# A transformer layer on one core: output products in 256-column pieces, rank offsets moved to TensorE, static expert transfers reordered

## The chip, the core and the metric

One core of a Trainium2 chip runs the whole kernel. The metric is the device time of one execution in microseconds, the median of several runs; the profile is of one further execution. Engines are named as the profile does: PE (TensorE), DVE (VectorE), ACT (ScalarE), POOL (GpSimd), SP (SyncE, which issues nearly all transfers).

## The reference

One layer on 256 tokens of width 1024, all float32: an adaptive modulation by a condition vector `c`, a mixer of two halves (a gated linear recurrence and an attention of 8 heads), a deepnorm residual, and a mixture of 32 experts of which each token takes two.

```python
mod = (silu(c) @ w_ada + b_ada).reshape(6, 1024)        # sh1, sc1, g1, sh2, sc2, g2
u   = normalize(x) * (1 + sc1) + sh1
proj = u @ w_in                                         # x_lru, y_lru, q, k, v
mix = concat(rmsnorm(rg_lru(conv(x_lru)) * gelu(y_lru)),
             rmsnorm(attention(q, k, v))) @ w_out
x   = layernorm(ALPHA * x + g1 * mix)
u2  = normalize(x) * (1 + sc2) + sh2
# router: best of 4 groups, best 2 of its 8 experts, weights from both softmaxes
hdn = silu(u2 @ w1[e]) * (u2 @ w3[e])                   # e: 32 experts, 1024 -> 256
ffn = sum over a token's two experts of weight * (hdn @ w2[e])
out = layernorm(ALPHA * x + g2 * ffn)
```

## The kernel before

The kernel is written in the order in which each engine is to run its instructions; nothing reorders them. The 256 tokens are two halves of 128 (`i` = 0, 1), one token to a partition. Products are float32 on PE; one of 512 columns is two recorded matmuls.

**First part.** Modulation columns, the input projection, the recurrence and the attention. Weights come in transfers of 1 MB, issued by SP one after the other; each waits until the buffer it writes is free, and everything behind it on SP waits too. `mod2_out`/`mod2_in` send two modulation vectors to memory and back in another shape, both on SP: `mod2_in` waits until `mod2_out` has landed. `vec_mm(4, q, pa2)` and `vec_mm(5, q, pa2)` (line 597) form the modulation rows sc2 and g2 from a 2 MB weight each; all go to one PSUM bank, `pa2`, and `vec_rows` (L608) reads the first half of it on DVE.

**Middle part**, where the change is. For each half of the tokens, `base(i, h)` multiplies the recurrence's rows by the upper part of `w_out` (columns `h`*512 on), `wo_mm(i, h, 1)` (L815) the attention's rows by the lower part, and `z_half` (L906 to L908) adds the second into `xt` and takes statistics of the sum; `x2_of` then applies the first layernorm. `logits` and `top` find each token's two experts (`om`, one-hot rows, and `mb`, their sum in bfloat16). A token's rank within its expert is `mb` of the tokens before it, summed by a product with a triangular matrix (`trib`, L1084 for half 0, L1140 to L1142 for half 1). `early_slots(i, ranks)` adds each expert's offset `v512` to the ranks (L1073) and turns them into the one-hot matrix `ohs[:, i]` (L1074 to L1077), and `early_rows(i)` (L1081) gathers the tokens' rows with it by TensorE into the columns of the first expert product `products(ph0, first, xs0)` (L1223). Between them stand `acc_init(i, h)` (L1111), products that put ALPHA times the residual into the four accumulators in which the result is summed later.

**The experts.** Six experts are chosen before the router has run, by the router's bias (`early_experts`). They are called static, and `statics((e, part), ...)` issues their weights (part 0, 1, 2 is w1, w3, w2, 1 MB each) from L870 into buffers as they come free: experts 0 to 4, and w2 of all six, into buffers of earlier weights, w1 and w3 of expert 5 into `fifth`, which takes the place of `mT` and `lnb`. The order of these calls in the program is SP's order. When half 1's router is done, DVE finds which other experts have tokens (to `eof`, L1192), SP loads their numbers into registers, and `bring_all` (L1177, L1180) issues their weights one after the other into the buffers of experts that have been used. The first such transfer overwrites w1 of expert 0, so it waits until `products(ph0, ...)` has used it. `unit` then runs eight groups of experts; the last ends with the second layernorm and the stores.

Two rules of the framework matter below. A wait is for a count of instructions that another engine has finished. A bank of PSUM is one tile for this purpose: who reads any part of it waits until the last write that stands ahead of the read in the program.

## Time and profile before

| | |
|---|---|
| median of 3 runs | 305.39 us (305.02 to 308.27) |
| profiled execution, its own time | 306.72 us |
| its span in the trace | 304.9 us |
| busy share of PE / DVE / ACT | 92% / 60% / 36% |
| transfers | 112.24 MB, mean 368 GB/s |
| granted TensorE clock, mean | 0.981 of full |

The profiled execution took 1.3 us more than the median of the timed runs, and 1.82 us of its time lie outside the span. All positions below are microseconds from the start of the span.

### The profile page before, as it was taken

How to read it: one execution, taken by the hardware profiler on the slowest of the kernel's cores; microseconds unless marked ns; L12 is line 12 of the kernel's file. 1: busy time of each engine (PE TensorE's matmuls, PEld its weight loads, DVE VectorE, ACT ScalarE, POOL GpSimd, SP SyncE). 2: the span in 40 equal slices, each digit the busy share in tenths (PEclk: the TensorE clock that was granted, in tenths of full speed). 3: DMA queues.
4: the chain of work that ended last, by engine and by line, in shares of the span. 5: the costliest groups of instructions: out<-in, count | busy, mean ns of one | idle time of the engine just before them, and what ended most of it. 6: DMA issues, size and time to landing. Idle time of an engine off the chain costs nothing.

```text
span 304.9 us, 6238 instructions
## 1 busy us (share of the span) xinstructions
PE 279.5 (92%) x2408; PEld 187.1 (61%) x2408; DVE 184.0 (60%) x450; ACT 109.2 (36%) x230; POOL 29.0 (9%) x60
## 2 busy tenths in 40 slices
PE   0699999999999999999979999999999999978980
PEld 0578887998867644565556568575647464824430
DVE  2684597728775866897797791545263616250392
ACT  1233569497556352150455331214112311220111
POOL 0100037700010000001020200000000000400000
PEclk9999999999999999999997999999999999997996
DMA  7999999999997999699889699999999999999304
GB/s 284 427 420 421 419 416 416 396 419 421 419 420 291 383 397 416 213 392 347 318 293 412 255 411 422 422 421 418 422 418 420 422 419 420 419 417 400 122 3 148
DMA packets 18740, 112.24 MB, mean 368 GB/s; under 512 B 2253, under 2 KB 3586, under 8 KB 6156
## 3 DMA queue, kind: packets, MB, share of 16 engines
q1 hardware_dynamic: 18000, 110.74, 89.8%
q10 hardware_dynamic: 636, 0.99, 0.9%
q8 instruction: 21, 0.34, 0.4%
q14 instruction: 19, 0.16, 0.2%
q0 software_dynamic: 64, 0.01, 0.0%
HBM read 110.51 MB, written 1.22 MB: 366 GB/s over the span
## 4 chain that ended last, share of the span: by engine, by line
PE 63%; DMA 20%; DVE 11%; ACT 2%; issue 1%; POOL 0%; SPq 0%; ACTq 0%; DVEq 0%
PE b L425 15%; DMA arena<-in_w 12%; PE m L1223 10%; PE b L815 7%; DMA misc<-in_w 7%; PE m L1366 5%; PE b L790 4%; PE m L1297 3%; PE a L589 2%; PE a L1223 2%; PE acc L1320 2%; PE a L372 2%; PE a L601 2%; DMA pka<-in_pack_a 2%; PE acc L1111 1%
## 5 line engine op out<-in xcount | busy, mean ns | idle before, releaser
L425 PE MATMUL b<-ul,w 128*128 128x256 f32 x384 | 49.4, 287 | 0.6 <-ACT w L405 0.5
L425 PEld LDWEIGHTS b<-ul,w 128*128 128x128 f32 x384 | 46.9, 192 | 4.7 <-ACT w L405 1.4
L1223 PE MATMUL m<-arena,xg 128*64 128x256 f32 (+1 forms) x288 | 38.4, 401 | 3.3 <-DMA arena<-in_w 3.3
L403 DVE TENSOR_TENSOR w<-arena,w 128x512 fp32r<-128x512 f32 x32 | 21.9, 701 | 14.9 <-ACT w L402 14.7
L1223 PEld LDWEIGHTS m<-arena,xg 128*64 128x64 f32 (+1 forms) x288 | 21.9, 130 | 13.6 <-DMA arena<-in_w 4.2
L1366 PE MATMUL m<-arena,hT 128*32 128x512 f32 (+2 forms) x184 | 29.1, 596 | 0.5 <-ACT hT L1344 0.5
L815 PE MATMUL b<-arena,mT 128*128 128x512 f32 x64 | 29.0, 601 | 0.1
L1338 DVE TENSOR_TENSOR hh<-hh,m 128x256 f32<-128x256 f32 x7 | 3.0, 421 | 34.2 <-ACT hh L1337 34.2
L1223 PE MATMUL m<-fifth,xg 128*32 128x256 f32 (+1 forms) x96 | 23.2, 401 | 0.0
L402 ACT ACTIVATE w<-arena 128x512 fp32r<-128x512 f32 x32 | 19.4, 626 | 6.4 <-PE b L425 5.3
L1223 PE MATMUL m<-misc,xg 128*32 128x256 f32 (+1 forms) x160 | 21.3, 380 | 0.0
L1379 ACT ACTIVATE yh<-ys 128x256 fp32r<-128x256 f32 (+1 forms) x22 | 10.5, 493 | 29.8 <-DVE ys L1378 25.9
L815 PEld LDWEIGHTS b<-arena,mT 128*128 128x128 f32 x64 | 11.6, 190 | 13.1 <-issue 12.6
L1378 DVE SCALAR_TENSOR_TENSOR ys<-m,ws,g2b 128x256 f32<-128x256 f32 (+1 forms) x22 | 12.0, 578 | 12.1 <-PE m L1366 11.9
L1337 ACT ACTIVATE hh<-m 128x256 f32<-128x256 f32 x7 | 2.7, 384 | 45.8 <-PE m L1223 45.8
L1366 PEld LDWEIGHTS m<-arena,hT 128*32 128x32 f32 (+2 forms) x184 | 8.5, 120 | 16.7 <-issue 13.5
L1297 PE MATMUL m<-oh,xa 128*128 128x256 f32 (+1 forms) x64 | 15.6, 284 | 0.0
L1297 PE MATMUL m<-oh,xb 128*128 128x256 f32 (+1 forms) x64 | 15.4, 281 | 0.0
L1223 PE MATMUL m<-last,xg 128*32 128x256 f32 x64 | 14.2, 380 | 0.0
L1223 PEld LDWEIGHTS m<-fifth,xg 128*32 128x32 f32 (+1 forms) x96 | 11.7, 124 | 3.5 <-issue 1.4
L1223 PEld LDWEIGHTS m<-misc,xg 128*32 128x32 f32 (+1 forms) x160 | 13.3, 126 | 0.8
L739 ACT ACTIVATE s<-s,z 128x128 f32<-128x128 f32 (+1 forms) x16 | 7.1, 448 | 18.2 <-DVE z L737 18.2
(316 smaller groups left out, 501.7 us busy)
## 6 DMA issues: line engine op xcount, KB each, us to landing
arena<-in_w SPq DMA_DIRECT2D x41, 1024.0 KB, 13.8
arena<-in_w_ada SPq DMA_DIRECT2D x22, 1024.0 KB, 14.6
arena<-in_w_in SPq DMA_DIRECT2D x10, 1024.0 KB, 15.2
last<-in_w SPq DMA_DIRECT2D x6, 1024.0 KB, 14.2
misc<-in_w SPq DMA_DIRECT2D x6, 1024.0 KB, 13.8
fifth<-in_w SPq DMA_DIRECT2D x6, 1024.0 KB, 14.8
arena<-in_w_out SPq DMA_DIRECT2D x4, 1024.0 KB, 9.0
arena<-in_w SPq DMA_DIRECT2D x8, 512.0 KB, 12.7
```

Source lines behind the costliest of these rows:

```text
L372: te.matmul(pa[32 * j:32 * j + 32, 0:128], cd[:, k], V1[v, a][:, k, j * 128:(j + 1) * 128], start=(k == 0), stop=(k == KD - 1), skip_group ...
L402: se.activation(t[:, 0], w[:, k], AF.Copy)
L403: ve.tensor_sub(t[:, 1], w[:, k], t[:, 0])
L425: te.matmul(half(bs, m), t[:, a, m * 128:(m + 1) * 128], ul[:, b, k], start=(k + m % 2 + a + b == 0), stop=(k == KD - 1 and a == 1), skip_ ...
L739: se.activation(s3[:, c], s3[:, c], AF.Exp, bias=z[:, c:c + 1], accum_out=z[:, 4 + c:5 + c])
L790: te.matmul(pvv[i], ul[:, ua, k, i * 128:(i + 1) * 128], t[:, wa], start=(k + wa + ua == 0), stop=(k == KD - 1 and wa == 1))
L815: te.matmul(p, mT[:, k, i * 128:(i + 1) * 128], wo[k // 4][:, k % 4, h * 512:(h + 1) * 512], start=(m == 0), stop=(m == 3))
L1223: te.matmul(ph[o:o + w, a * 256:(a + 1) * 256], xs[:, k, o:o + w], place[q][0].rearrange("p (a k f) -> p a k f", a=2, k=KD)[:, a, k], star ...
L1297: te.matmul(q, nhl[i][:, a, k * 128:(k + 1) * 128], oh[:, i, :n], start=(a + i == 0), stop=(a + i == 2))
L1366: te.matmul(ps[h][o:o + w], hT[:, j, o:o + w], place[q][1][:, j * 1024 + h * 512:j * 1024 + (h + 1) * 512], start=(j == 0), stop=(j == 1), ...
L1378: ve.scalar_tensor_tensor(ys[:, o:o + q], p[:, o:o + q], ws, g2b[:, sl], op0=OP.mult, op1=OP.mult)
L1379: se.activation(yh[:, sl], ys[:, o:o + q], AF.Copy)
```

## The change

It does seven things.

- `w_out` is stored with its 512-column halves apart, so that the first MB of each part holds the columns of `h` = 0 for all rows and the second those of `h` = 1, where before each MB held all columns of half the rows. The static transfers that overwrite it can then be issued half by half.
- The output products of half 1, `wo_mm(1, h, 1)`, run as two pieces of 256 columns. Between the two pieces of `h` = 0 stands the triangular product for half 0's ranks (L1084 before).
- The offsets `v512` come into the ranks by a product of a row of ones with `v512` on PE, ahead of the triangular product in the same sum, in place of the addition on DVE (L1073). Half 1's ranks with offsets get columns of their own (96 to 128).
- `early_slots(0)` on DVE stands ahead of both `z_half(1, h)`. `z_half(1, 1)` works in two pieces of 256 columns, and the statistics of half 1 are taken over pieces of 256.
- `vec_mm(5, 0)` moves up, to behind `vec_mm(4, 1)`; `pv_mm(1, 0)` moves down behind `vec_mm(5, 1)`.
- `acc_init(1, 1)` moves from ahead of `early_rows(1)` to behind `products(ph0, ...)`.
- On SP, `mod2_in(rows0)` moves behind the loads of the two g2 weights and of the layernorm rows, and the static transfers come in another order.

```diff
-    r["w_out"] = np.stack([wo[:, 4 * j:4 * j + 4].reshape(128, 4096) for j in range(2)])
+    r["w_out"] = np.stack([wo[:, 4 * j:4 * j + 4].reshape(128, 4, 2, 512).transpose(0, 2, 1, 3).reshape(128, 4096) for j in range(2)])
...
-    mod2_in(mod2_out(rows1[64:128:32], 0), 0)
+    rows0 = mod2_out(rows1[64:128:32], 0)
...
-    def wo_mm(i, h, part, pool=None):
+    def wo_mm(i, h, part, pool=None, halves=(slice(0, 512),), mid=None):
         p = bank(pool)
-        for m in range(4):
-            k = 4 * part + m
-            te.matmul(p, mT[:, k, i * 128:(i + 1) * 128], wo[k // 4][:, k % 4, h * 512:(h + 1) * 512],
-                      start=(m == 0), stop=(m == 3))
+        for n, q in enumerate(halves):
+            if mid and n:
+                mid()
+            for m in range(4):
+                te.matmul(p[:, q], mT[:, 4 * part + m, i * 128:(i + 1) * 128], wo[part][:, h, m, q],
+                          start=(m == 0), stop=(m == 3), skip_group_check=len(halves) > 1)
         return p
...
     ve.memset(lg, NEG)
+    mod2_in(rows0, 0)
...
+    def z_half(i, h, b, st, mv, parts=None):
+        w = D // st.shape[1]
+        for q in parts or (slice(0, 512),):
+            o = slice(h * 512 + q.start, h * 512 + q.stop)
+            t = tmp.tile([128, 512], F32, name="s")[:, q]
+            ve.scalar_tensor_tensor(t, b[:, q], ra[:, i:i + 1], g1b[:, o], op0=OP.mult, op1=OP.mult)
+            ve.tensor_add(xt[:, i, o], xt[:, i, o], t)
+            for c in range(o.start, o.stop, w):
+                ve.bn_stats(st[:, c // w], xt[:, i, c:c + w])
...
     vec_mm(4, 1, pa2)
+    vec_mm(5, 0, pa2)
     rows2 = mod2_out(vec_rows(4, pa2)[0:128:32], 1)
     statics((1, 0), (1, 1))
     mod2_in(rows2, 1)
+    statics((2, 0), (2, 1))
...
-    vec_mm(5, 0, pa2)
-    statics((2, 0), (2, 1))
-    pv_mm(1, 0)
     vec_mm(5, 1, pa2)
...
     statics((3, 0), (3, 1))
+    pv_mm(1, 0)
     pt(1, 2)
     norm(1, 3)
     base(1, 0)
+    statics((0, 2))
...
     pl0 = raw_mm(0, zT0)
+    te.matmul(pl0[:, 64:96], onesf[0:1], v512[0:1], start=True, stop=False, skip_group_check=True)
     constants_mm()
...
-    statics((4, 0), (4, 1), (0, 2), (1, 2))
+    statics((4, 0), (4, 1), (1, 2))
     rms_cols(row, ra[:, 1:2], psp)
-    bs = [wo_mm(1, 0, 1, psx)]
+    bs = [wo_mm(1, 0, 1, psx, quarters, lambda: te.matmul(pl0[:, 64:96], trib, mb[:, 0], start=False, stop=True,
+                                                          skip_group_check=True))]
+    statics((2, 2))
...
-        ve.tensor_add(s2[:, i], ranks, v512)
-        ve.tensor_mul(omv[:, :, i], om[:, :, i], s2[:, i:i + 1].to_broadcast([128, 2, NE]))
+        ve.tensor_mul(omv[:, :, i], om[:, :, i], ranks[:, None, :].to_broadcast([128, 2, NE]))
...
-    te.matmul(pl0[:, 64:96], trib, mb[:, 0], start=True, stop=True)
-    bs.append(wo_mm(1, 1, 1, psx))
-    zs = z_start()
+    bs.append(wo_mm(1, 1, 1, psx, quarters))
+    early_slots(0, pl0[:, 64:96])
+    zs = z_start(4)
     z_half(1, 0, bs[0], *zs)
-    early_slots(0, pl0[:, 64:96])
     pgs = [bank(psp) for _ in range(2)]
     early_rows(0)
-    statics((2, 2), (3, 2))
-    z_half(1, 1, bs[1], *zs)
+    statics((3, 2))
+    z_half(1, 1, bs[1], *zs, quarters)
...
-    statics((4, 2), (5, 0), (5, 1), (5, 2))
+    statics((5, 0), (5, 1), (4, 2), (5, 2))
...
     p = bank(psp)
+    te.matmul(p[:, 96:128], onesf[0:1], v512[0:1], start=True, stop=False)
+    te.matmul(p[:, 96:128], oneb, mb[:, 0], start=False, stop=False)
+    te.matmul(p[:, 96:128], trib, mb[:, 1], start=False, stop=True)
...
-    for h in range(2):
-        acc_init(1, h)
+    acc_init(1, 0)
...
-    early_slots(1, rk[:, 1])
+    early_slots(1, p[:, 96:128])
...
     products(ph0, first, xs0)
+    acc_init(1, 1)
```

Where the instructions stand, at three places. First DVE at half 1's sum: `s<-b` is the output product times its scale, `xt<-xt,s` the addition, `bst` or `bsz` the statistics, `omv`, `sl` and `wsd` the slots of half 0. In brackets are the engines whose counts an instruction waits for. Before:

```order
L908 BN_STATS bst<-xt 128x6 [waits DVE_49]
L1073 TENSOR_TENSOR s_1643<-b,v_709 128x32 [waits PE_49]
L1074 TENSOR_TENSOR omv<-keepers,s_1643 128x2x32 [waits DVE_49]
L1075 TENSOR_REDUCE sl_1642<-omv 128x2 [waits DVE_49]
L1076 TENSOR_SCALAR wsd<-pkb,sl_1642 128x128 [waits DVE_49]
L1077 SCALAR_TENSOR_TENSOR wsd<-pkb,sl_1642,wsd 128x128 [waits DVE_49]
L906 SCALAR_TENSOR_TENSOR s<-b,ra,xb 128x512 [waits PE_49]
L907 TENSOR_TENSOR xt<-xt,s 128x512 [waits DVE_49]
L908 BN_STATS bst<-xt 128x6 [waits DVE_49]
```

The same place on DVE in the changed kernel:

```order
L1087 TENSOR_SCALAR wsd<-pkb,sl_1649 128x128 [waits DVE_49]
L1088 SCALAR_TENSOR_TENSOR wsd<-pkb,sl_1649,wsd 128x128 [waits DVE_49]
L913 SCALAR_TENSOR_TENSOR s<-b,ra,xb 128x512 [waits PE_49,Pool_49]
L914 TENSOR_TENSOR xt<-xt,s 128x512 [waits DVE_49]
L916 BN_STATS bsz<-xt 128x6 [waits DVE_49]
L916 BN_STATS bsz<-xt 128x6
L913 SCALAR_TENSOR_TENSOR s<-b,ra,xb 128x256 [waits PE_49]
L914 TENSOR_TENSOR xt<-xt,s 128x256 [waits DVE_49]
L916 BN_STATS bsz<-xt 128x6 [waits DVE_49]
L913 SCALAR_TENSOR_TENSOR s<-b,ra,xb 128x256
L914 TENSOR_TENSOR xt<-xt,s 128x256 [waits DVE_49]
L916 BN_STATS bsz<-xt 128x6 [waits DVE_49]
```

The slots stand ahead of the sum; the three operations on the second 512 columns have become six on 256. The first 256-column operation waits for PE and the second has no wait for PE of its own: both read one bank, and the one wait is for the last of the products written to it.

Second, PE around `vec_mm`: `a<-arena,cd` and `a<-last,cd` are the g2 products (16 matmuls to one `vec_mm`), `b<-arena,mT` the output products, `b<-pka,misc` transposes of the attention. Before:

```order
L601 MATMUL a<-arena,cd 32x256 x16
L760 MATMUL b<-pka,misc 128x128 x4
L808 MATMUL b<-avg,row 128x1
L815 MATMUL b<-arena,mT 128x512 x4
L760 MATMUL b<-pka,misc 128x128 x4
L725 MATMUL b<-nx 128x256 x4
L815 MATMUL b<-arena,mT 128x512 x8
L601 MATMUL a<-arena,cd 32x256 x16
L772 MATMUL b<-misc,xb 64x128 x8
L601 MATMUL a<-last,cd 32x256 x16
L1033 MATMUL a<-misc,pka 32x256 x4
L760 MATMUL b<-pka,misc 128x128 x4
```

The same place on PE in the changed kernel:

```order
L601 MATMUL a<-arena,cd 32x256 x32
L760 MATMUL b<-pka,misc 128x128 x4
L808 MATMUL b<-avg,row 128x1
L817 MATMUL b<-arena,mT 128x512 x4
L760 MATMUL b<-pka,misc 128x128 x4
L725 MATMUL b<-nx 128x256 x4
L817 MATMUL b<-arena,mT 128x512 x8
L601 MATMUL a<-last,cd 32x256 x16
L1040 MATMUL a<-misc,pka 32x256 x4
L772 MATMUL b<-misc,xb 64x128 x8
L760 MATMUL b<-pka,misc 128x128 x4
```

Sixteen g2 matmuls have moved ahead of three output products (12 of 512 columns); the work up to the last row is the same.

Third, PE from the ranks of half 1 to the gather `b<-wsd,nx`: `acc` is an `acc_init`. Before:

```order
L1141 LDWEIGHTS oneb
L1141 MATMUL b<-mb,oneb 128x32
L1142 LDWEIGHTS trib
L1142 MATMUL b<-mb,trib 128x32
L1111 MATMUL acc_1702<-xt,aid 128x512
L1111 MATMUL acc_1703<-xt,aid 128x512
```

The same place on PE in the changed kernel:

```order
L1154 LDWEIGHTS oneb
L1154 MATMUL b<-mb,oneb 128x32
L1155 LDWEIGHTS trib
L1155 MATMUL b<-mb,trib 128x32
L1121 MATMUL acc_1715<-xt,aid 128x512
L1092 MATMUL b<-wsd,nx 128x128 x8
```

One of the two `acc_init` is gone from ahead of the gather.

## Rows read from the trace of the kernel before

**Rows 1.** The page, part 2: memory traffic in 40 slices of 7.62 us.

```profile
GB/s 284 427 420 421 419 416 416 396 419 421 419 420 291 383 397 416 213 392 347 318 293 412 255 411 422 422 421 418 422 418 420 422 419 420 419 417 400 122 3 148
```

**Rows 2.** The chain that ended last: start, duration, what.

```profile
128.92 0.59 PE b L760 x4
...
142.80 3.54 PE b L815 x8
...
148.66 0.10 DVE s L1073
...
149.97 0.72 DVE s L906
...
152.17 0.22 DVE bmv L896
...
159.91 0.20 DVE mb L993
...
160.40 3.51 PE acc L1111 x4
163.91 1.78 PE b L1081 x16
165.69 7.17 PE a L1223 x128
...
182.47 6.92 PE m L1223 x32
...
219.50 15.74 DMA arena<-in_w
...
275.54 8.78 PE m L1223 x122
```

**Rows 3.** SP's timeline: transfers issued, start and duration.

```profile
97.89 0.86 SPq L233 DMA_DIRECT2D arena<-in_w_ada  x2
...
169.30 1.64 SPq L1177 DMA_DIRECT2D arena<-in_w  x3
```

**Rows 4.** SP's waits, 160 to 176 us: sum, times, longest.

```profile
SPq L1177 <- PE a L1223: 2.3, 2, 1.7
```

**Rows 5.** Windows of 4 us: busy by engine, PE clock, DMA share, GB/s.

```profile
168.00:172.00 4.00, 4.00 (x80) 2.44 (x76) 3.52 (x9) 0.19 (x1) 1.43 (x3) 1.00 0.43 124
...
276.00:280.00 4.00, 4.00 (x48) 2.08 (x44) 0.00 (x0) 0.00 (x0) 0.00 (x0) 0.57 1.03 401
```

**Rows 6.** DVE's groups by form: busy us, mean ns; idle before, releaser.

```profile
L1378 DVE SCALAR_TENSOR_TENSOR ys<-m,ws,g2b 128x256 f32<-128x256 f32 x14 | 6.1, 479 | 4.2 <-PE m L1366 4.1
...
L1385 DVE TENSOR_TENSOR yl<-ys,yh 128x256 fp32r<-128x256 f32 x14 | 5.3, 419 | 0.0
...
L906 DVE SCALAR_TENSOR_TENSOR s<-b,ra,xb 128x512 f32<-128x512 f32 x4 | 3.0, 751 | 4.6 <-PE b L815 2.4 <-PE b L1084 2.2
...
L907 DVE TENSOR_TENSOR xt<-xt,s 128x512 f32<-128x512 f32 x4 | 2.8, 692 | 0.1
```

**Rows 7.** DVE's timeline: start, duration.

```profile
126.52 0.70 DVE L750 TENSOR_TENSOR misc<-s,z 128x512 f32<-128x512 f32 x1
...
142.10 0.19 DVE L993 TENSOR_TENSOR mb<-keepers 128x32 bf16<-128x32 f32 x1
...
163.66 0.15 DVE L1192 TENSOR_SCALAR eof<-eid 128x1 int32<-128x1 f32 x1
164.91 1.37 DVE L1209 TENSOR_SCALAR xt<-b,mod2p 128x128 f32<-128x128 f32 x4 [1.10 <-PE b L1081]
```

**Rows 8.** PE's timeline: start, duration (recorded twice for each float32 matmul).

```profile
123.67 1.93 PE L601 MATMUL a<-arena,cd 128*32 128x256 f32 x32
...
134.11 0.38 PE L972 MATMUL b<-wsum,onesf 128*128 128x36 f32 x2
134.42 0.41 PE L973 MATMUL b<-pkb,onesf 1*128 1x36 f32 x2
```

**Rows 9.** PE in windows of 0.5 us: busy, granted clock, DMA share, GB/s.

```profile
163.00:163.50 0.50, 0.50 (x2) 0.50 1.08 459
```

More of the change, by code (lines that the diff above doesn't have):

```diff
@@ L248, in load_wo @@
     def load_wo(j, s):
-        return load(s, w_out[j], 4)
+        return load(s, w_out[j], 4).rearrange("p (h a) (b n) -> p h (a b) n", h=2, b=2)
     se.dma_start(pka, pack_a)
@@ L898, in bn_end, with z_start @@
         return mv, rs
-    def z_start():
-        return tmp.tile([128, 2, 6], F32, name="bst"), tmp.tile([128, 2], F32, name="bmv", bufs=4)
-    def z_half(i, h, b, st, mv):
-        sl = slice(h * 512, (h + 1) * 512)
-        t = tmp.tile([128, 512], F32, name="s")
-        ve.scalar_tensor_tensor(t, b, ra[:, i:i + 1], g1b[:, sl], op0=OP.mult, op1=OP.mult)
-        ve.tensor_add(xt[:, i, sl], xt[:, i, sl], t)
-        ve.bn_stats(st[:, h], xt[:, i, sl])
+    def z_start(n=2):
+        return tmp.tile([128, 4, 6], F32, name="bsz")[:, 0:n], tmp.tile([128, 2], F32, name="bmv", bufs=4)
+    quarters = (slice(0, 256), slice(256, 512))
+    def z_half(i, h, b, st, mv, parts=None):
[7 more added lines that the diff above has]
+                ve.bn_stats(st[:, c // w], xt[:, i, c:c + w])
     def x2_of(i, mv, rs):
```

## The prediction

> **What bounds the kernel now.** I read the memory traffic first [rows 1]: from slice 23, at 175 us, to slice 35 it stands at 409 to 422 GB/s without a gap. In the chain that ended last [rows 2] the pieces from 219.50 are transfers, and PE's last expert starts at 275.54, when its weights have landed. So the end comes a fixed time after the first transfer of a router-chosen expert. It is issued at 169.30 [rows 3]; SP stood ready and waited up to 1.7 us for PE [rows 4], for the first half of `products(ph0)`: that starts at 165.69 and takes 7.17 [rows 2], so its first half ends at 169.28. Between 168 and 172 memory moves only 124 GB/s [rows 5]: the static transfers are through, nothing else may start. Hence one number decides: how far **the start of `products(ph0)`** moves. Before it the chain [rows 2] is PE to the end of the output products (142.80, twice 3.54, the small triangular product between: 149.93), DVE from 149.97 to half 1's experts (159.91 + 0.20), then PE: two `acc_init` (3.51), the gather (1.78).
>
> **`vec_mm(5, 0)` earlier.** Its 16 matmuls, 1.86 us (32 of the recorded ones fill 123.67 to 125.60 [rows 8]), now stand ahead of three output products. PE's sum up to the transposes at 128.92 [rows 2] stays, but DVE gets its inputs 1.86 later. Those transposes need DVE's L750, done at 126.52 + 0.70 = 127.2 [rows 7]; now 129.1, so PE waits near 0.1. The same lateness follows through the next transposes and ACT's copies, which I put at another 0.1. Bounds: 0.1 and 0.5; I take **+0.2**. Its weight is asked for at 97.89 [rows 3]; 2 MB at 420 GB/s are 5 us, and the product now starts near 111, so it is there. DVE's lateness also reaches `mb` of half 0, ready at 142.29 [rows 7]; even with 1.86 on it that is 144.15, and PE reaches the triangular product, now in the middle of the first output product, at 142.80 + 1.77 = 144.57. Covered; what it costs without the cover is a rival below.
>
> **Offsets by PE, half 0.** A product of one row by 32 columns is added on PE's path. The nearest rows are two small ones whose starts are 0.31 apart [rows 8]: **+0.3**, bounds 0.1 and 0.4.
>
> **Output products in pieces.** Eight products of 512 columns, 0.885 each (3.54 for four), become 16 of 256. The trace has 16 full-array products of 256 columns in 6.92 [rows 2], 0.433 each, weight loads hidden. So 16 pieces cost 6.92 where the eight cost 7.08: **-0.1**, bounds -0.16 and +0.2. Together PE ends these products 0.4 later, near 150.3.
>
> **Slots of half 0 ahead of the sum.** On DVE they filled 148.66 to 149.97 [rows 2], and moving them looks like 1.3 us. But PE's last output product ends at 149.93 and DVE starts on it at 149.97: both came at the same time. The gain is **0.04**; DVE is only ready earlier and waits for PE.
>
> **The sum in pieces on DVE.** Could it start on the first 256 columns while PE makes the second? In the order of the changed kernel the first piece waits for PE and the second has no wait, so the one wait covers the bank's last product. DVE thus starts where it did, with six operations instead of three. The three took 152.17 - 149.97 = 2.20 [rows 2], 0.73 a step. An operation of 256 columns is shorter by 0.27 (0.751 against 0.479, 0.692 against 0.419 [rows 6]), so a step is 0.46 and six are 2.78: **+0.58**. For statistics of 256 columns no row exists; between half their 0.70 and all of it the bounds are +0.4 and +1.1, and I stay with the two forms that were measured. [...] The statistics of the first 512 columns are split too, but DVE has near 1 us to spare there.
>
> So DVE reaches half 1's statistics, and by unchanged steps its experts, 0.4 + 0.58 = **1.0 later**, at 161.1.
>
> **Offsets by PE, half 1.** The addition, a step of about 0.22 on DVE, goes; three more small products stand among those that DVE waits for, at 0.03 to 0.1 each. **-0.15**, bounds -0.23 and +0.1. So DVE's list of experts `eof`, done at 163.81 [rows 7], comes at 164.66. SP needs it, but has 1.7 us to spare [rows 4].
>
> **`acc_init(1, 1)` away from the gather.** [...] In the profile's own clock: the remaining one starts 1.05 later than at 160.40 and takes 1.75, so the gather can start at 163.2 instead of 163.91. But if the slow stretch, 160.4 to 163.75 in the profile, is only moved by the same 1.05, it lasts to 164.8, and 1.6 us of the gather run at half speed, doing 0.8 of its 1.78. It ends at 165.8: **+0.1** against 165.69. With full clock before and after: before, the gather would end at 163.95 and DVE's first copies of it, behind `eof`, at 164.15; after, `eof` at 164.66 puts them at 165.0: **+0.9**. So what this edit saves, the pieces have spent, or it saves nothing since DVE's list of experts is later than the gather.
>
> Behind `products(ph0)` it costs PE 0.88, and PE's experts come that much later. The cover is the transfer queue: at 219.50 a transfer needs 15.74 us to land [rows 2], so PE frees buffers long before they are reached. Without it the price is 0.88.
>
> **SP's new order, the layout of `w_out`.** The same bytes. The gaps that earlier static transfers fill are paid back at 168 to 172, where the queue is empty anyway: **0**. The last ones, for `fifth`, wait for DVE's `x2_of(1)`, which is 1.0 later; 4 MB after that are 10 us and end near 168, still before the first chosen transfer. If not, the queue has no gap there and nothing is lost.
>
> **The sum.** The profiled execution took 306.72, the median of the runs is 305.39; whether the timed runs had the half-clock stretch isn't shown. Between +0.1 and +0.9 I take +0.5: **305.9**. With the bounds of the terms (0.4 less, 0.9 more) the main case reaches from 305.0 to 307.0.
>
> **Rivals.**
> *The clock stays up.* PE's idle times in the changed kernel lie a little differently. If the stretch at 160 to 163.7 runs at full clock where it didn't, `products(ph0)` starts at 165.0 to 165.1, 0.6 earlier than in the profile; if the one at 276 to 280 (0.57 [rows 5]) goes too, where 122 recorded matmuls took 8.78 and 128 at full clock take 7.17 [rows 2], another 1.7. Times 303.1 to 304.8. For it: both stretches follow idle time of PE, and the first idle time is split in two by DVE's later sum. Against: the longer part of it, while DVE finds half 1's experts, stays as long. [...] Chance 0.17.
> *The pieces do overlap.* If the first piece could start at DVE's own readiness, 149.4, the two end at 152.2 instead of 153.2, and the kernel is 1.0 better than forecast: 304.9. For it: the split has no other use. Against: the wait in the order. Chance 0.07.
> *DVE's lateness reaches PE*, the slower side. If `mb` of half 0 comes more than 2.3 us later than 142.29, PE waits in the middle of the output products, and everything behind waits too. 1.86 from the moved product, PE's own 0.5 and a longer stall in ACT's copies make that possible. With all of 1.86 on PE's path and the pieces' 0.58 on DVE's, less 0.15 and with a full clock, it is +2.3 to +3.1: 307.7 to 308.5. Against: DVE waits for PE again at `base(1, 0)`, which absorbs 0.65. Chance 0.09.
> *The transfers were the brake.* If earlier static transfers let the chosen ones start earlier, the 4 us at 124 GB/s [rows 5] hold 2.8 us: 302.6. Against: SP waits for PE, not for a transfer [rows 4]. Chance 0.03.
>
> **How the numbers follow.** Main case 0.60, the rivals 0.36 together, 0.04 for the rest. Range 303.7 to 307.3: the main case, the overlap, and most of the clock's case; what is left out is the slower rival and the ends, about 0.2. One per cent, 3 us, is about what a measurement here can tell from no change. Faster by more: the clock's lower end, the transfers and half of the rest, 0.06. Slower by more: the upper end of the slower rival and the rest, 0.06. Within it: 0.88.
>
> **What the profile of the changed kernel would show.** The first 256-column piece on DVE starts within 0.1 us after the last output product and six steps take 2.7 to 2.9; the slots of half 0 end near 146.5; a wait of PE before the transposes of L760 near 129; half 1's `mb` near 161.1; `eof` near 164.7; `products(ph0)` between 165.0 and 165.9 and the first chosen transfer 3.6 after it; traffic without a gap from there. A first piece that starts while PE still multiplies, a PE wait at the triangular product, or a first chosen transfer that waits for a transfer would make the prediction wrong, and so would a gap in the traffic after 175.

## The result and the profile after

| | before | changed |
|---|---|---|
| median of 19 runs each, us | 305.70 (304.76 to 309.62) | 307.95 (304.96 to 309.86) |
| ratio, 95% interval | | 1.0057 (1.0033 to 1.0081) |
| profiled execution, its span, mean clock | 306.72, 304.9, 0.981 | 307.95, 306.1, 0.992 |

The ratios, and below the differences of medians that have an interval, leave out runs more than 1.5% above the fastest of their kernel, and the ratios are not quotients of the medians shown. By the ratio's interval the change makes the kernel slower by 1.0 to 2.5 us. I had forecast 305.9; the median lies 0.65 above the upper end of my range.

The two profiled executions can't be laid over each other from the start of the span. The chain of the changed kernel begins like this (start, duration, what; only unchanged code):

```profile
13.93 3.62 PE a L372 x64
...
23.87 1.89 PE a L372 x64
...
101.47 1.14 DVE mT L860 x4
```

The same form of 64 products takes 3.62 us the first time and 1.89 later. In the kernel before it takes no longer the first time (PE's timeline), and the second row answers to the last one above:

```profile
13.87 1.95 PE L372 MATMUL a<-arena,cd 128*32 128x128 f32 x64
...
99.85 1.14 DVE mT L858 x4
```

So 1.62 us of the difference lie ahead of the change. Over the 20 executions profiled for this case that copy stands at 99.50 to 101.71, a spread of 2.21 us. What slows the first products isn't shown: the profile's windows give full clock there (1.00 from 12 to 20 us), and no run shows what causes the spread. **From here on positions are counted from the start of that copy**, and written p: in the kernel before, `products(ph0)` is at 165.69 - 99.85 = p 65.84 [rows 2] and the first chosen transfer at p 69.45 [rows 3].

The chain of the changed kernel through the middle part:

```profile
135.82 0.64 PE b L760 x4
136.50 0.33 issue
136.82 0.61 ACT misc L762
...
140.47 0.33 PE b L1057 x2
...
145.43 1.83 PE b L817 x8
147.28 5.29 PE b L817 x24
152.59 0.49 DVE s L913
...
155.34 0.27 DVE bmv L899
...
163.13 0.20 DVE mb L1001
...
165.05 3.33 PE b L1092 x16
168.37 7.04 PE a L1235 x128
...
278.37 7.09 PE m L1235 x122
```

Against [rows 2]: the output products end at 152.57, p 51.10 against p 50.08, so PE is **1.0 later** there (forecast 0.4). The pieces themselves cost nothing: 1.83 + 5.29 with the triangular product between them, 7.12, against 7.13. DVE aggregates the statistics at p 53.87 against 52.32 (**+1.55**); `mb` ends at p 61.85 against 60.25 (+1.6, forecast 1.0); `products(ph0)` starts at p 66.90 against 65.84 (**+1.06**, forecast 0.5). The gather takes 3.33 where it took 1.78. PE in windows of 4 us (the last three columns are PE's granted clock, the DMA share and GB/s):

```profile
164.00:168.00 4.00, 3.72 (x17) 2.98 (x16) 3.38 (x14) 2.39 (x8) 0.00 (x0) 0.57 1.01 424
...
276.00:280.00 4.00, 2.12 (x34) 1.04 (x37) 1.41 (x5) 0.00 (x0) 0.00 (x0) 1.00 1.00 403
```

In these two executions the half-clock stretch (a granted clock of 0.50 in windows of 0.5 us, from 160.50 to 163.50 before and from 164.50 to 167.50 after) lies on the two `acc_init` before [rows 9] and on the gather after; before, the gather has a clock of 1.00 from 164.00 on. That place isn't the change's doing alone: the gather takes 2.82 in e1, which is the kernel before again, and 2.41 in e10, the changed kernel again. Ahead of the stretch PE had been idle, waiting for half 1's `mb`:

```profile
163.38 0.18 PE L1150 MATMUL b<-mb,trib 128*128 128x32 bf16 x1 [1.64 <-DVE mb L1001]
```

At the last expert, where [rows 5] has 0.57, this execution has full clock, hence 7.09 instead of 8.78 there. So the two profiles don't show the loss as it is in the medians: of the 1.2 us between their spans, 1.62 come ahead of p 0 and 1.21 up to the last expert (p 176.90 against 175.69), and 1.69 are given back in it. SP's timeline, which answers to [rows 3]:

```profile
171.97 2.30 SPq L1189 DMA_DIRECT2D arena<-in_w  x3
174.65 0.33 SPq L1189 DMA_DIRECT2D last<-in_w  x1
...
181.71 4.21 SPq L1192 DMA_DIRECT2D arena<-in_w  x4
```

The first chosen transfer is at p 70.50, **1.05 later**, 3.60 behind `products(ph0)` as before (3.61).

### The profile page after: what moved, and what is told of

Same layout as the page of the kernel before. It is cut to its first block, busy times and chain, and to the rows that moved or that the text cites. A ratio compares the mean times of both kernels' runs of the same rounds, so it can differ in the third digit from the quotient of the medians.

```text
span 306.1 us, 6282 instructions
## 1 busy us (share of the span) xinstructions
PE 280.5 (92%) x2430; PEld 192.0 (63%) x2430; DVE 184.2 (60%) x452; ACT 109.5 (36%) x230; POOL 29.0 (9%) x60
## 4 chain that ended last, share of the span: by engine, by line
PE 62%; DMA 20%; DVE 13%; ACT 2%; issue 1%; POOL 0%; SPq 0%; ACTq 0%; DVEq 0%
PE b L425 15%; DMA arena<-in_w 12%; PE m L1235 9%; PE b L817 7%; DMA misc<-in_w 6%; PE m L1379 5%; PE b L790 4%; PE a L372 3%; PE m L1310 3%; PE a L589 2%; PE a L1235 2%; PE acc L1333 2%; DMA pka<-in_pack_a 1%; PE b L628 1%; PE a L601 1%
## 5 line engine op out<-in xcount | busy, mean ns | idle before, releaser
L1235 PE MATMUL m<-arena,xg 128*64 128x256 f32 (+1 forms) x288 | 36.7, 380 | 2.8 <-DMA arena<-in_w 2.8
L817 PE MATMUL b<-arena,mT 128*128 128x512 f32 (+1 forms) x80 | 29.1, 514 | 0.1
L1235 PEld LDWEIGHTS m<-arena,xg 128*64 128x64 f32 (+1 forms) x288 | 21.2, 125 | 12.2 <-DMA arena<-in_w 4.0
L1235 PE MATMUL m<-fifth,xg 128*32 128x256 f32 (+1 forms) x96 | 21.5, 380 | 0.0
L817 PEld LDWEIGHTS b<-arena,mT 128*128 128x128 f32 x80 | 14.6, 190 | 10.8 <-issue 9.6
```

The source lines that it names most:

```text
L817: te.matmul(p[:, q], mT[:, 4 * part + m, i * 128:(i + 1) * 128], wo[part][:, h, m, q], start=(m == 0), stop=(m == 3), skip_group_check=len ...
L1235: te.matmul(ph[o:o + w, a * 256:(a + 1) * 256], xs[:, k, o:o + w], place[q][0].rearrange("p (a k f) -> p a k f", a=2, k=KD)[:, a, k], star ...
```

## The experiments

Theory A: the end follows `products(ph0)`, and that follows DVE, which is late by three additive costs. Theory B: half-clock stretches that the change brings carry most of the loss. Theory C: the order of transfers, or `acc_init(1, 1)` behind `products(ph0)`, costs. Theory D, for the combined version: what is won ahead of `products(ph0)` is lost behind it. All positions are of the one profiled execution of each kernel; a dagger marks one without a stretch at half clock between `mb` and `products(ph0)`. The last column is the ratio to the kernel before, run on the same chip; the kernel before had medians of 305.1 to 305.8 beside them.

| run | aggregation | `mb` ends | `ph0` | first chosen | last expert | median | ratio, 95% interval |
|---|---|---|---|---|---|---|---|
| before | 52.32 | 60.25 | 65.84 | 69.45 | 175.69 | 305.70 | |
| changed | 53.87 | 61.85 | 66.90 | 70.50 | 176.90 | 307.95 | 1.0057 (1.0033 to 1.0081) |
| e1 before again | 52.30 | 60.23 | 65.78 | 69.38 | 175.45 | 305.72 | 1.0009 (0.9982 to 1.0037) |
| e2 sum whole | 53.38 | 61.30 | 66.07 | 69.67 | 177.17 | 307.02 | 1.0064 (1.0042 to 1.0087) |
| e3 g2 back | 53.32 | 61.31 | 66.69 | 70.29 | 176.64 | 307.33 | 1.0083 (1.0046 to 1.0120) |
| e4 two banks † | 52.67 | 60.73 | 64.67 | 68.34 | 174.26 | 307.47 | 1.0078 (1.0050 to 1.0107) |
| e5 fill † | 53.88 | 61.86 | 65.80 | 69.47 | 175.97 | 307.34 | 1.0059 (1.0028 to 1.0090) |
| e6 before, fill † | 52.33 | 60.26 | 64.37 | 68.05 | 174.36 | 305.98 | 1.0004 (0.9981 to 1.0028) |
| e7 three back | 52.36 | 60.29 | 65.07 | 68.67 | 175.91 | 306.79 | 1.0024 (0.9992 to 1.0055) |
| e8 before, acc † | 52.31 | 60.24 | 64.36 | 68.03 | 173.59 | 305.95 | 0.9994 (0.9961 to 1.0028) |
| e9 combined † | 51.65 | 59.70 | 64.12 | 67.79 | 173.78 | 306.68 | 1.0029 (1.0002 to 1.0056) |
| e10 changed again | 53.90 | 61.88 | 66.57 | 70.17 | 176.65 | 307.62 | 1.0068 (1.0039 to 1.0096) |
| e11 before, order | 52.33 | 60.26 | 65.81 | 69.41 | 175.53 | 305.69 | 0.9994 (0.9966 to 1.0021) |
| e12 offset 0 on DVE | 53.43 | 61.41 | 66.67 | 70.27 | 176.21 | 307.14 | 1.0030 (1.0001 to 1.0059) |
| e13 before, end † | 52.31 | 60.23 | 64.36 | 68.03 | 173.86 | 304.82 | 0.9986 (0.9957 to 1.0015) |
| e14 both fills † | 53.89 | 61.87 | 65.81 | 69.48 | 175.82 | 305.87 | 0.9994 (0.9962 to 1.0026) |
| e15 combined, end † | 51.65 | 59.70 | 63.64 | 67.31 | 174.35 | 305.10 | 0.9978 (0.9945 to 1.0011) |
| e16 before, fills † | 52.33 | 60.26 | 64.38 | 68.05 | 174.38 | 305.53 | 0.9984 (0.9947 to 1.0020) |
| e17 changed, end | 53.88 | 61.86 | 67.13 | 70.74 | 177.62 | 307.70 | 1.0054 (1.0026 to 1.0083) |
| e18 before, delay † | 52.32 | 60.24 | 65.46 | 69.06 | 175.12 | 307.87 | 1.0057 (1.0024 to 1.0090) |

### How much is chance

e1 is the kernel before and e10 the changed one, with no edit.

> The kernel before once more, for the clock of each of its runs and for the size of chance. Theory A (the changed kernel is late because DVE reaches half 1's statistics 1.55 us later, and products(ph0) with it): its runs show the same spread of granted clocks as those of the changed kernel, of which 7 of 19 lie under 0.985, and the ratio to the kernel before is 1.000 within 0.0025. Theory B (the clock: the change makes half-clock stretches more frequent, and these carry most of the 1.7 us): at most 3 of its runs lie under 0.985.

> The changed kernel once more, on the same chip as the other three. Theories A and B: 1.5 to 1.9 above the kernel before. Chance (the ratio of the first comparison was drawn high): 0.5 to 1.2 above it.

The result repeats: 1.0068. Runs of one kernel differ by 2 to 7 us, so an edit worth 0.5 us is read from positions here, not from a median. The clock sign of the first expectation tells nothing: under 0.985 stood 3 of 12 runs in e1, as theory B had it, but also only 2 of 12 in e10. At the upper end there is a difference. A mean granted clock of 0.994 or more had 53 of 155 runs of the kernel before taken beside the others and 5 of 31 of the changed kernel, which luck alone could still make. With e1, e8 and e11 it is 64 of 191; with the versions of the changed kernel that add no products (e2, e3, e4, e7, e12) it is 9 of 83. So the first half of theory B holds: the changed kernel and its versions have such a clock less often.

### Edits undone one at a time

In e2 DVE's last sum is whole again:

```diff
-    zs = z_start(4)
+    zs = z_start(2)
...
-    z_half(1, 1, bs[1], *zs, quarters)
+    z_half(1, 1, bs[1], *zs)
```

> The changed kernel with z_half(1, 1) on DVE in one piece and its statistics over 512, as before; PE's products stay in pieces. Theory A: from DVE's first copy at L860 (start of the copies into mT) to half 1's aggregation it is 53.3 us instead of 53.87 in the changed kernel, products(ph0) starts 0.5 earlier, and the time is 0.4 to 0.6 below the changed kernel, 1.0 to 1.2 above the kernel before. Theory B: the aggregation moves as well, but the time stays within 0.2 of the changed kernel in runs of the same clock.

The aggregation moves by 0.49, as theory A has it. The time doesn't follow: its median is 1.9 above the kernel before beside it, not 1.0 to 1.2. In e3 the g2 product and what moved with it go back:

```diff
-    vec_mm(5, 0, pa2)
     rows2 = mod2_out(vec_rows(4, pa2)[0:128:32], 1)
...
-    statics((2, 0), (2, 1))
...
+    vec_mm(5, 0, pa2)
+    statics((2, 0), (2, 1))
+    pv_mm(1, 0)
     vec_mm(5, 1, pa2)
...
-    pv_mm(1, 0)
```

> The changed kernel with vec_mm(5, 0), pv_mm(1, 0) and the static transfers (2, 0), (2, 1) at their places of before. Theory A: PE no longer waits for L750 ahead of the transposes L760 (0.31 and 0.15 in the changed kernel), the output products end 0.5 to 0.6 earlier, the aggregation stands at 53.3 instead of 53.87 from the first copy at L860, and the time is 0.5 lower. My prediction had put this edit at 0.2. Theory C (the static transfers' new order is the cost): the output products end where they did, and what moves is the first chosen transfer against products(ph0).

The aggregation moves by 0.55. PE's timeline of the changed kernel shows what the edit had cost (in brackets the idle time before, and its releaser):

```profile
130.71 0.63 PE L760 MATMUL b<-pka,misc 128*128 128x128 f32 x4 [0.31 <-DVE misc L750]
...
135.82 0.63 PE L760 MATMUL b<-pka,misc 128*128 128x128 f32 x4 [0.15 <-DVE misc L750]
...
137.47 1.09 PE L772 MATMUL b<-misc,xb 128*64 128x128 f32 x14 [0.18 <-ACT misc L762]
```

and the same three rows in e3, with none of the three waits:

```profile
130.20 0.66 PE L760 MATMUL b<-pka,misc 128*128 128x128 f32 x4
...
135.02 0.60 PE L760 MATMUL b<-pka,misc 128*128 128x128 f32 x4
...
136.11 1.63 PE L772 MATMUL b<-misc,xb 128*64 128x128 f32 x16
```

The time doesn't follow in e3: the stretch lies on the gather (3.65 in its chain), and the nine runs include three above 310. In e12 half 0's offset goes back to DVE:

```diff
-    te.matmul(pl0[:, 64:96], onesf[0:1], v512[0:1], start=True, stop=False, skip_group_check=True)
...
+            ve.tensor_add(s2[:, i], ranks, v512)
```

> The changed kernel with half 0's offset added by DVE again, the product of one row ahead of the triangular one gone. My prediction had put that product at 0.3 on PE's path. Theory A: the output products end 0.33 to 0.45 earlier and the aggregation stands at 53.4 to 53.5 from the first copy at L860 instead of 53.87; the time falls by 0.4. If PE's path is set there by DVE and ACT instead, the aggregation moves by less than 0.1.

The aggregation moves by 0.44; the ratio, 1.0030, is lower than the changed kernel's, as theory A has it, within intervals too wide to tell. e7 undoes all three.

> The changed kernel with three edits undone together: DVE's sum whole, vec_mm(5, 0) with pv_mm(1, 0) and statics (2, 0), (2, 1) in their old places, half 0's offset by DVE again. Kept: the slots ahead of the sum, PE's products in pieces, half 1's offset by PE, acc_init(1, 1) behind products(ph0), the other order of transfers. Theory A: the aggregation is back at 52.3 from the first copy at L860, and the time is that of the kernel before or 0.2 below it. Theory B: the aggregation is back too, but with the half-clock stretch on the gather the time is still 0.5 to 1.0 above the kernel before.

0.49 + 0.55 + 0.44 = 1.48; together they move it by 1.51, to the place of before. The three costs add up, and there is no fourth ahead of DVE's aggregation. In time, e7 is between theories A and B: its interval holds both no loss and 1.7 us.

### Why the pieces don't overlap

```diff
-    bs.append(wo_mm(1, 1, 1, psx, quarters))
+    bs.append([wo_mm(1, 1, 1, psx, (q,)) for q in quarters])
...
-    z_half(1, 1, bs[1], *zs, quarters)
+    for b, q in zip(bs[1], quarters):
+        z_half(1, 1, b, *zs, (q,))
```

> The changed kernel with the two 256-column pieces of wo_mm(1, 1, 1) in two PSUM banks. If the wait for the whole bank is what keeps the pieces on DVE from overlapping (theory A), the first piece on DVE starts 1.1 earlier, right after the statistics of the first 512 columns, while PE still multiplies; the aggregation stands at 52.8 to 52.9 from the first copy at L860 instead of 53.87, and the time is 1.0 below the changed kernel, 0.5 to 0.8 above the kernel before. If the pieces lose by their number alone, or DVE is late for another reason, the aggregation stays within 0.2 of 53.87.

DVE's timeline, first the changed kernel:

```profile
150.72 0.75 DVE L916 BATCH_NORM_STATS2 bsz<-xt 128x6 f32<-128x256 f32 x2
152.59 0.48 DVE L913 SCALAR_TENSOR_TENSOR s<-b,ra,xb 128x256 f32<-128x256 f32 x1 [1.12 <-PE b L817]
```

then the version with two banks:

```profile
149.29 0.75 DVE L916 BATCH_NORM_STATS2 bsz<-xt 128x6 f32<-128x256 f32 x2
149.96 0.47 DVE L913 SCALAR_TENSOR_TENSOR s<-b,ra,xb 128x256 f32<-128x256 f32 x1
```

and PE's there, with the output products' last 24 records and the gather that follows them:

```profile
145.70 5.43 PE L817 MATMUL b<-arena,mT 128*128 128x256 f32 x24
150.96 1.95 PE L1092 MATMUL b<-wsd,nx 128*128 128x128 f32 x16
```

With its own bank the first piece starts at 149.96, while PE multiplies until near 151. The wait of 1.12 us is gone and the aggregation is 1.2 earlier. The expectation on the time failed: 307.47 in seven runs, 2.4 above the kernel before, though `products(ph0)` and the last expert stand earlier than those of the kernel before. None of the seven reaches a mean clock of 0.994.

### The order of transfers, and acc_init alone

e11 is the kernel before with the new order of transfers and the new layout of `w_out`; e8 has one edit:

```diff
-    for h in range(2):
-        acc_init(1, h)
+    acc_init(1, 0)
...
     products(ph0, first, xs0)
+    acc_init(1, 1)
```

> The kernel before with the new order of transfers alone: the halves of w_out apart, mod2_in behind the loads of the g2 weights, the statics in the changed order where the edits on PE don't move them. Theory A: the aggregation and products(ph0) stand where they did, the time within 0.3 of the kernel before. Theory C (the order costs): 0.5 to 1.0 above the kernel before, which would be what is left of the loss in the kernel with three edits undone.

> The kernel before with one edit: acc_init(1, 1) behind products(ph0). Theory A (the edit is a gain, as far as the clock or DVE's eof let it): products(ph0) 0.1 to 0.8 earlier than 65.84 from the first copy at L860, the time 0 to 0.6 below the kernel before. Theory C (it is a loss: PE's experts come later behind products(ph0), and with them the transfers of w2, which in the changed kernel follow the first chosen one by 9.73 us instead of 9.15): the time is 0.3 to 0.6 above the kernel before, and w2's first transfer follows the first chosen one by 9.7.

Neither costs anything that can be measured, with intervals of about 1 us either way. In e8, w2 follows the first chosen transfer by 9.73 us instead of 9.15, as theory C says, but the last expert stands no later for it (p 173.59, the earliest of all) and the time stays. Nor does it gain: without a stretch `products(ph0)` is at p 64.36 with the edit, and at 64.36 to 64.38 without it (e6, e13, e16).

### The clock

Three products of 256 columns fill PE's idle time ahead of `mb` (e5, and e6 from the kernel before):

```diff
+    for _ in range(3):
+        te.matmul(acc[1][1][:, 0:256], aid, x2[:, 1, 0:256], start=True, stop=True, skip_group_check=True)
```

> The changed kernel with three more products of 256 columns on PE (1.3 us) in its idle time ahead of half 1's mb; they write an accumulator that acc_init(1, 1) sets anew later, so the output is the same. Theory B (the half-clock stretch that falls on the gather is a main part of the loss, because an idle PE stands ahead of it and acc_init no longer covers it): no stretch at half clock between mb and products(ph0), the gather takes 1.8 us instead of 3.33, products(ph0) starts at 65.3 to 65.5 from DVE's first copy at L860 instead of 66.90, and the time falls by 1.0 to 1.5, to 306.0 to 306.5 by the level of the kernel before of 305. Theory A (DVE's lateness alone): the time stays within 0.3 of the changed kernel.

> The kernel before with the same three products in the same idle time. Theory B: here the stretch falls on the two acc_init, and DVE's eof covers most of it, so products(ph0) starts at 65.0 to 65.2 from the first copy at L860 instead of 65.84 and the time falls by no more than 0.6. Theory A: no change beyond 0.2.

The positions are as expected: no stretch there, and `products(ph0)` 1.1 earlier in the changed kernel, 1.47 in the other. All four executions with this fill (e5, e6, e14, e16) are without the stretch; of the fifteen with nothing more in that idle time, five are too. The time hardly follows: the median of e5 is 0.9 below that of the changed kernel, with an interval of -1.7 to +0.8, and e6 is no faster than the kernel before. Five more products fill the waits for the last weights (e13 and e17 alone, e14 and e16 with the other fill):

```diff
+            def busy(j):
+                for _ in range((0, 0, 2, 3)[j]):
+                    te.matmul(dum[:, 0:256], ident, srow[:, 0:256], start=True, stop=True)
```

> The kernel before with five products of 256 columns more in the last expert's products: two (0.9 us) ahead of the third group's first product and three (1.3 us) ahead of the fourth's, where PE waits 1.42 and 1.87 for weights. They go to a bank that nobody reads. Theory B (the half-clock stretch at the last expert costs 1.7 to 2.9 us where it comes): no such stretch, the last expert's 122 recorded products take 7.1 instead of 8.78, and the time is 0.3 to 0.9 below the kernel before. If that stretch isn't caused by PE's wait there, it stays, and so does the time.

> The changed kernel with the five products in the last expert alone. If the stretch at the last expert is what costs the changed kernel the rest (theory B for that place), the time is 1.0 to 1.7 below the changed kernel, near 306.2 to 306.6 with the kernel before at 305.4; if both stretches are needed for it, 0.3 to 0.8 below it. The tail from the last expert's start to the end is 27.7 us in the profile, without a stretch.

> The changed kernel with both idle times filled: three products of 256 columns ahead of half 1's mb, and the five in the last expert. Theory A: no half-clock stretch ahead of the end, products(ph0) at 65.8 from the first copy at L860, and the time 1.2 to 1.6 above that of the kernel before with the same two fills (e16_before_fills), which is the cost by positions alone. Theory B (the clock carries most of the loss): within 0.8 of it.

> The kernel before with both idle times filled as in e14_both_fills. Theory B: no half-clock stretch ahead of the end, and the time is 0.4 to 1.0 below the kernel before. Theory A says nothing on it but that e14_both_fills stays 1.2 to 1.6 above.

Windows of PE in e14 (PE's clock, DMA share, GB/s last):

```profile
164.00:168.00 4.00, 3.81 (x52) 1.00 1.03 428
...
276.00:280.00 4.00, 3.86 (x72) 1.00 1.03 407
```

The changed kernel falls by 1.9 us with both fills (95% interval 1.0 to 2.6), by 0.9 with the first alone and by 0.1 with the second alone. (These are differences of medians, the intervals from redrawing the runs.) The kernel before gains 0.4 with the end fill and loses 0.3 with both, both within their intervals of none. All five executions with the end fill have full clock at the last expert, 7.09; so have five of the fifteen without it. Of the timed runs of the changed kernel each fill alone leaves most below a clock of 0.994 (9 of 12 in e5, all 12 in e17), both fills 4 of 12 (e14); of the kernel before it is 11 with the first (e6), 4 with the second (e13) and 2 with both (e16).

e14 against e16 was to part theory A, 1.2 to 1.6, from theory B, below 0.8. It gives +0.3 (interval -0.5 to +0.9), theory B's side, where their positions at the last expert differ by 1.44; against e13 it is +1.05 (0.1 to 1.9). Runs of equal clock say something else: at 0.994 or more the 5 of the changed kernel have a median of 306.43 and the 53 of the kernel before 305.02, 1.4 apart (0.5 to 1.9), which is the size of the difference in positions, and the remaining 1.1 of the 2.5 between all their runs would be the clock's. That sorting was done after the fact and rests on five runs. So the clock is a part of the loss; whether it is 1 us or nearly all of it isn't settled: of the runs that were timed there is a mean clock, not the places of their stretches.

### A later products(ph0) and nothing else

```diff
+    te.matmul(acc[1][1][:, 0:256], aid, x2[:, 1, 0:256], start=True, stop=True, skip_group_check=True)
+    acc_init(1, 1)
     ph0 = abank()
     products(ph0, first, xs0)
```

> The kernel before with 1.3 us of products on PE between the gather and products(ph0): one of 256 columns into an accumulator, and acc_init(1, 1) once more, which sets it anew. Nothing else differs. Theory A (the end follows products(ph0)): it starts 1.3 later, at 67.1 from the first copy at L860 with a stretch there, the first chosen transfer too, and the time is 1.2 to 1.5 above the kernel before, 306.6 to 306.9. Theory B on top of it (a later start also brings more stretches at the last expert): 1.7 to 2.2 above, with fewer than a quarter of the runs at a clock of 0.994 or more. If SP or the transfers have slack there, less than 0.8.

The chain of this run:

```profile
163.54 1.81 PE b L1081 x16
165.34 0.43 PE acc L1228 x2
165.78 0.86 PE acc L1111 x2
166.64 7.17 PE a L1223 x128
...
276.30 8.78 PE m L1223 x122
```

`products(ph0)` stands at p 65.46, 1.1 later than in the executions of before without a stretch, and the last expert 0.7 to 1.5 later (p 175.12 against 173.59 to 174.38 in e6, e8, e13 and e16). The ratio is 1.0057, that of the changed kernel. A delay at this one place, with none of the edits, gives a loss of the same size. But the median is 2.1 above the kernel before for a delay of 1.1, and only 1 of 12 runs reaches a clock of 0.994, against 7 of 23 beside it. That is what theory B on top of A had forecast (1.7 to 2.2); the interval, 0.7 to 2.8, holds theory A's 1.2 to 1.5 as well.

### Two versions put together

e9 and e15 have two banks, the g2 product back and half 0's offset on DVE; e9 also moves `acc_init(1, 1)` ahead of `mb`, e15 has the five products at the end.

> A version that keeps what the runs so far spoke for: the two 256-column pieces of wo_mm(1, 1, 1) in two PSUM banks, vec_mm(5, 0) with pv_mm(1, 0) and statics (2, 0), (2, 1) in their old places, half 0's offset by DVE, slots ahead of the sum, half 1's offset by PE, and acc_init(1, 1) in PE's idle time ahead of half 1's mb (acc_init(1, 0) stays behind the ranks). Theory A (the end follows products(ph0)): from the first copy at L860 the aggregation stands at 51.6 to 51.8 (52.32 before), mb ends at 59.6, products(ph0) starts at 63.4 to 63.8 (65.84 before, 64.4 without a half-clock stretch there), and the time is 0.5 to 1.0 below the kernel before. Theory D (what is won there is lost behind it, in the first 12 us of the chosen transfers or to the clock): products(ph0) is as early, but the time is that of the kernel before, within 0.3.

> The changed kernel with the two pieces in two banks, vec_mm(5, 0), pv_mm(1, 0) and statics (2, 0), (2, 1) in their old places, half 0's offset by DVE, and the five products in the last expert. Theory A with B: the aggregation at 51.65 from the first copy at L860 (52.32 before), mb ends at 59.6, products(ph0) starts at 63.7 to 64.0 (64.4 in the kernel before where no stretch comes), no stretch at the last expert, and the time is 0.8 to 1.4 below the kernel before. If something behind products(ph0) takes the gain, the time is within 0.4 of the kernel before.

By the medians e9 is 1.3 us above the kernel before (0.1 to 1.7 by the ratio's interval), where theory A had a gain and theory D at most 0.3; its last expert takes 10.04 and none of its runs reaches 0.994. In e9 the move costs 0.5 between `mb` and DVE's `eof`: 4.02 against 3.54 in e15. e15's `products(ph0)` is the earliest of all, p 63.64, but its last expert starts at 174.35, no earlier than in e16: from the first chosen transfer it takes 107.04 us instead of 106.33. Its time is 0.6 below the kernel before by the medians, short of theory A's 0.8 to 1.4. Neither it nor e13, whose medians are the lowest, can be told from the kernel before.

## Why the prediction was wrong

**Two steps failed**: the way from the edits to `products(ph0)` was priced too low, and what the change does to the clock was put at nothing. I forecast +0.5 on a median of 305.39 and got +2.25 on one of 305.70. Of the 2.05 missing, 0.3 is the level of the kernel before and 0.6 to 0.9 is `products(ph0)`, which comes 1.06 to 1.43 later instead of 0.5. The rest, 0.8 to 1.2, is not in that position.

**What decides** was right as a chain of positions: the start of `products(ph0)` sets the first chosen transfer, 3.6 us later, and that the start of the last expert, within a microsecond or two. That a delay there alone makes the kernel slower, e18 shows; how much of the time it carries isn't settled. Right were also the steps on the rest of SP's order (0; e11), `acc_init` behind `products(ph0)` (e8), half 0's slots (DVE then waits 1.12 for PE), and half 1's offset (from `mb` to `eof` 3.54 instead of 3.71, -0.17; forecast -0.15).

**The sum in pieces**: the whole-bank wait was right (e4), and six steps take 152.59 to 155.34, 2.75 (forecast 2.78); +0.49 in e2 against +0.58. Statistics of 256 columns, for which I had no row, take 0.43, and the addition of 256 columns takes 0.42, as in [rows 6].

**Two terms were mis-sized.** *vec_mm(5, 0) earlier*: +0.2, measured 0.55, just outside my bounds of 0.1 to 0.5. I put the first wait for L750 at 0.1 and all that follows at another 0.1; the waits are 0.31, then 0.15 when PE overtakes DVE again at the next transposes, and 0.18 for ACT's copy of these. *Offsets by PE, half 0*: +0.3, measured 0.44, above its bound of 0.4 too; 0.33 of it is the product itself. With -0.1 for PE's pieces that were 0, PE ends 1.0 later, not 0.4, and `mb` is 1.6 later, not 1.0. The bounds were also added up too kindly: those of the five terms come to 0.6 less and 1.5 more, not 0.4 and 0.9, and with the +0.9 that I had for full clock the main case would have reached 307.8.

**From mb to products(ph0)**: the sum took +0.5 for `products(ph0)`, the middle between +0.1 in the profile's clock and +0.9 at full clock. With `mb` 1.6 later both ends rise: +1.06 with a stretch, and +1.43 at full clock (65.80 against 64.37, e5 and e6), there bound by `eof` as I had said. Without a stretch one `acc_init` takes 0.86 and the gather 1.81 (e18). My sign for it, 165.0 to 165.9, is p 65.15 to 66.05; in three executions of the changed kernel's middle part (changed, e10, e17) it is 66.57 to 67.13. I had moved the stretch by DVE's lateness, which makes the gather 2.6; it takes 3.33 here, 2.41 in e10 and 3.55 in e17, so the stretch has no place that one profile could give.

**The clock** was put at nothing: the sum took the stretches of the kernel before as those of the changed one, and my one rival on it made the kernel faster. Instead the changed kernel and its versions reach a mean clock of 0.994 in 9 of 83 runs where the kernel before and its versions do in 64 of 191, and with products in both idle times the changed kernel gains 1.9 us though `products(ph0)` is still 1.43 late. Why its clock is lower is open.

**Constant after the first chosen transfer** holds only within a microsecond or two. From it to the last expert it is 105.6 to 106.3 us in eight executions of the kernel before and its versions, 105.9 to 107.5 in twelve of the changed kernel's, 0.5 more in the mean. In the changed kernel's rows above, SP takes 3.01 us for the first four issues. In the kernel before it takes 2.34, from 169.30 [rows 3] to the end of

```profile
171.31 0.33 SPq L1177 DMA_DIRECT2D last<-in_w  x1
```

But e18 takes 3.6 for them and is at 106.06. What causes the difference is open.

**The rivals.** The pieces didn't overlap. The transfers weren't the brake. The clock didn't stay up ahead of `products(ph0)`. The time fell where I had put DVE's lateness reaching PE (307.7 to 308.5), but not by its mechanism, so that is luck: the triangular product in the middle of the output products didn't wait; two small terms and the clock added up instead. Two readings of mine were off without consequence: from slice 23 the traffic is 411 to 422 GB/s, not 409, and the row of 32 recorded g2 products [rows 8] gives 1.93, not 1.86.

## What to carry to other kernels

When an operation is moved ahead on one engine, follow the engine that gets its inputs late through every later exchange between the two, not only the first; each stall is small and they add (here 0.31, 0.15 and 0.18 us). Splitting a producer into pieces buys nothing while the consumer's wait covers the whole bank: give each piece a bank, as in e4, where a wait of 1.12 us went, or leave it whole. Where a chain is read against another execution, count from an event in unchanged code, test a chain's claim by a plain delay at the place in question, and compare the clocks of the timed runs before giving the whole loss to positions.

## What the hardware showed that I had not expected

The same code starts 2.2 us earlier or later from one execution to the next (p 0 at 99.50 to 101.71), and a stretch at half clock (0.50 from 276.50 to 279.50 in the kernel before) after an idle time of PE (1.86 us there) can cost as much as the change: the last expert's products take 7.09 us without one and 8.60 to 10.04 with one. None of the four executions with 1.3 us of idle products ahead of `mb` has a stretch between `mb` and `products(ph0)`, but only with the second idle time filled as well does the changed kernel gain, 1.9 us; 8 of the 12 runs of e14 then have a granted clock of 0.994 or more, against 5 of 31 of the changed kernel.
